# The gate and early merge weights of a two-layer hybrid encoder: their loads issued by ScalarE instead of SyncE

## The chip, the cores and the metric

The kernel runs on one core of a Trainium2 chip. A core has a matrix engine (TensorE, PE in the profile; its weight loads are PEld), VectorE (DVE), ScalarE (ACT), GpSimd (POOL) and SyncE (SP), which here only issues DMA transfers. Each engine executes its own instructions in order, and semaphores tie the engines together. ScalarE and GpSimd can issue DMA transfers too, as instructions among their others. The metric is the time of one execution on the device in microseconds (us); three executions of the kernel before took 3136.10, 3140.98 and 3143.68 us, median 3140.98.

## What is computed

Two layers of a bidirectional encoder trunk, sequence 2048, width 1024, float32. Cut to what matters:

```
for l in range(2):
    h = rms_norm(x, norm_w[l])
    qkv, z_a, a_lg, b_lg, cf_val, cf_glu, z_b, gate_lg = split(h @ w_in[l])
    # branch A: short convolution + SiLU on q, k, v; normalised q, k; the gated
    # delta rule in chunks of 64, forward and backward, both summed:
    #   v_new = value - k_cum @ S;  o = q_dec @ S + attn @ v_new
    #   S = S * decay + k_dec^T @ v_new
    o = rms_norm_per_head(o_fwd + o_bwd) * silu(z_a)
    y_a = o @ w_dn_out[l]
    # branch B: GLU, convolution of width 31, LayerNorm, SiLU, gated
    y_b = (u * silu(z_b)) @ w_cf_out[l]
    gate = sigmoid(gate_lg + gate_b)          # 2 x 1024 wide
    x = x + (gate[0] * y_a + gate[1] * y_b) @ w_out[l]
return rms_norm(x, final_norm_w)
```

The change concerns the weights of `gate_lg` (the last 2048 columns of `w_in`) and of `w_cf_out`.

## The kernel before

**Dense products.** A product of two float32 operands is made of three matrix products on reduced-precision parts: each operand is split into a high part and the rest, and PE forms high by high (L185), rest by high (L186) and high by rest (L187). A weight tile has 1024 (for `w_cf` 512) input rows and 128 output columns. `weight_parts` loads it in blocks of 512 rows, 128x512 numbers or 256 KB each, into the tile `wraw` (two buffers), so a gate weight takes two loads and a `w_cf` weight one. `split` then forms `whi` with a copy on ScalarE (L159) and `wlo` with a subtraction on VectorE (L160); both have two buffers. `weight` is `weight_parts` followed at once by the split. `load` and `store` issue on SyncE's queue (L147, L150), `astore` on ScalarE's (L153), `pstore` on GpSimd's.

**Stages of a layer.** First the input products with the short convolution, then the Conformer branch and the products of z. Then come the *early gates*, `gates(0)`: the gate products of the first half of the sequence, between which VectorE and GpSimd work on the Conformer convolution and its norm and on the triangular solves of the recurrence. Then `delta()`, the recurrence of branch A, in 16 steps, each for both directions. Last comes the merge with the rest of `w_cf`, with `w_dn` and `w_out`.

**The recurrence and its filler.** The steps of the recurrence are chains of small operations across PE, ScalarE and VectorE, so dense products are put between them as filler: `pull(n)` takes n pieces from a generator. `filler` first gives `gates(1)`, the gate products of the second half of the sequence, and after them `early_merge`, which multiplies half of branch B by `w_cf` and by its gate. A few pieces go into the *lead-in* ahead of step 0 (`LEAD`), 16 into each step (`STEP`, four times four), the rest behind. After delta(), `bind` makes the written order binding for PE, ScalarE, VectorE and GpSimd, while SyncE's loads are free to go ahead in the order that the scheduler found.

**A gate product** is 24 matmuls into a bank `pd` of PSUM (three banks), which ScalarE empties with the bias into `go` (L829); `astore` writes that to memory as `gt`. The recurrence's own results go into banks `pz`, five in turn.

**Lines of the recurrence that the text speaks of.** PE: L936 and L946 in the preparation of a later step; L989 and L992 apply the state, L1005, L1014 and L1023 give the step's output and the state's increment. ScalarE: L925 and L963 in the preparation, L939 there too, L998 and L1007 in the step itself. VectorE: transposes L917 and copies L971 and L972 in the preparation, L1017 for the state's update. When both directions of a pair of chunks are there (steps 8 to 15), `finish` squares their sum on ScalarE (L1044), forms the norms' factors with small operations on VectorE (from L1054), has the scaled sum transposed by PE into `pz`, and multiplies it by the z gate on VectorE (L1068), which empties that bank. In steps 8 to 11 (`LATE_SQUARES` = 12) these squares come ahead of the third `pull` of the step, later behind it:

```
            if step < LATE_SQUARES:
                next(new)
            pull(STEP[2])
            if step >= LATE_SQUARES:
                next(new)
```

Of the kernel before, what the change touches and what calls it, by code (L numbers as in the profile page):

```python
# [19 lines left out]
KD = 8  # L20
# [39 lines left out]
def sort(ps):  # L60
    return ps.rearrange("p (i a) -> p a i", a=2)


def cut(x):
    return x.rearrange("p (a i) -> p a i", a=2)
# [13 lines left out]
class Trunk:  # L79
# [78 lines left out]
    def split(self, hi, lo, src):  # L158
        self.nc.scalar.activation(hi, src, AF.Copy)  # L159
        self.nc.vector.tensor_tensor(out=lo, in0=src, in1=hi.bitcast(F32), op=ALU.subtract)  # L160

    def weight_parts(self, src, kk):
        hi = self.pw.tile([P, KD, P], F32R, tag="whi", bufs=2, name="whi")[:, 0:kk, :]
        lo = self.pw.tile([P, KD, P], F32R, tag="wlo", bufs=2, name="wlo")[:, 0:kk, :]
        raws = []
        for k in range(0, kk, 4):
            raws.append(self.pw.tile([P, 4, P], F32, tag="wraw", bufs=2, name="wraw"))
            self.load(raws[-1], src[:, k:k + 4, :])

        def split():  # L170
            for k, raw in zip(range(0, kk, 4), raws):
                self.split(hi[:, k:k + 4, :], lo[:, k:k + 4, :], raw)
        return (hi, lo), split

    def weight(self, src, kk):
        w, split = self.weight_parts(src, kk)
        split()
        return w

# [630 lines left out]
    def gates(self, half):  # L810
        nc = self.nc
        seq = [(j, b) for j in range(16) for b in range(2)]
        if half:
            seq = seq[:28] + [(14, 0), (15, 0), (14, 1), (15, 1)]
        ws = {}
        for i, (j, b) in enumerate(seq):
            for q, _ in seq[i:]:
                if q not in ws and len({z for z, _ in seq[i:] if z in ws}) < 2:
                    ws[q] = self.weight(self.a["w_in"][self.l, 28 + q], KD)
            blk = 2 * half + b  # L820
            ps = self.pd()
            for more in self.dense_steps(ps, ws[j], self.hx(blk), KD):
                if more:
                    yield 1
            if self.rate:
                self.follow()
                self.pump(self.rate)
            o = self.st("go")
            nc.scalar.activation(cut(o), sort(ps), AF.Identity if half else AF.Sigmoid,  # L829
                                 bias=self.vec[:, V_GB + j:V_GB + j + 1])  # L830
            self.astore(self.gt_d[j, :, blk * NB:(blk + 1) * NB], o)
            yield 1
# [321 lines left out]
    def filler(self):  # L1154
        wcf = self.a["w_cf"][self.l]
        seq = [(j, b) for j in range(KD) for b in range(2)]
        u = ahead = None
        gs = deque()

        def gate(i):  # L1160
            j, b = seq[i]
            t = self.st("g1")
            self.load(t, self.gt_d[8 + j][:, b * NB:(b + 1) * NB])
            gs.append(t)

        def units():
            yield from self.gates(1)
            self.u0 = u
            self.y1 = self.big([P, KD, HALF], F32, "y1")
            yield from self.early_merge(wcf, ahead, seq, gs, gate)  # L1170

        for n, v in enumerate(units()):
            yield v
            if n == 30 * KD - 1:
                self.drain()
                self.rate = 0.0
                u = self.big([P, 8, HALF], F32R, "uop")
                raw = lambda k, b: u[:, 4 + k, b * NB:(b + 1) * NB]
                for b in range(2):
                    for k in range(4):  # L1180
                        self.load(raw(k, b).bitcast(F32), self.u_d[k, :, b * NB:(b + 1) * NB])
                gate(0)
            if n == 31 * KD - 1:
                ahead = self.weight(wcf[0], 4)
                gate(1)
            if n in SPLITS:
                b, k = divmod(SPLITS.index(n), 4)
                self.split(u[:, k, b * NB:(b + 1) * NB], raw(k, b), raw(k, b).bitcast(F32))

    def early_merge(self, wcf, ahead, seq, gs, gate):  # L1190
        nc = self.nc
        for i, (j, b) in enumerate(seq):
            if b == 0:
                wc = ahead
                if j + 1 < KD:
                    ahead, split = self.weight_parts(wcf[j + 1], 4)
            elif j + 1 < KD:
                split()
            if i + 2 < len(seq):
                gate(i + 2)  # L1200
            g = gs.popleft()
            sl = slice(b * NB, (b + 1) * NB)
            ps = self.pd()
            for more in self.dense_steps(ps, wc, lambda k: (self.u0[:, k, sl], self.u0[:, 4 + k, sl]), 4):
                if more:
                    yield 1
            nc.vector.tensor_tensor(out=cut(self.y1[:, j, sl]), in0=sort(ps), in1=cut(g), op=ALU.mult)
            yield 1
# [291 lines left out]
```

## Time and profile before

| | before |
|---|---|
| median of three executions | 3140.98 us (3136.10 to 3143.68) |
| profiled execution | 3143.1 us |
| its span in the profile | 3141.3 us |
| mean granted clock of TensorE | 0.995 |
| busy PE / DVE / ACT / POOL | 3077.3 / 2400.3 / 1377.3 / 297.9 us |

The page gives busy time of each engine over the span. A row of the waits reads: engine, its tile and line, then the engine, tile and line that ended the wait; total us, times, longest. A row of the timeline reads: start in us from the start of the span, duration, engine, line, operation, out<-in with shapes, and how many instructions are drawn together; a wait ahead of it stands in brackets, with what ended it. ACTq and SPq are the issuing sides of the two DMA queues. A row of the transfers gives the number of issues, the size of one and the median time from issue to landing.

### The profile page before, as it was taken

The numbers are of one execution on the slowest core, as the hardware profiler recorded it, in microseconds if no ns is written. First come the engines' busy times: TensorE is split into PE (matmuls) and PEld (weight loads), VectorE is DVE, ScalarE is ACT, GpSimd is POOL, SyncE is SP. The second block draws the span as 40 slices with busy tenths as digits, with TensorE's granted clock in tenths as the row PEclk, the third lists the DMA queues.
The fourth block names the chain that finished last, engine by engine and source line by source line (L and its number), as shares of the span: only waits on it lengthen the run. The fifth ranks groups of instructions, "written<-read, shape, count | busy, mean of one in ns | idle before, by whom it ended". The sixth has DMA issues, their size and how long they took to land. (4 is left out here: it accounts for less than half of the span.)

```text
span 3141.3 us, 51438 instructions
## 1 busy us (share of the span) xinstructions
PE 3077.3 (98%) x19190; PEld 2707.1 (86%) x19190; DVE 2400.3 (76%) x4441; ACT 1377.3 (44%) x3074; POOL 297.9 (9%) x297
## 2 busy tenths in 40 slices
PE   6999999999999999999999999999999999999998
PEld 5888888888889998888888888888888899988887
DVE  7789898997556698746666989999955567877665
ACT  5625152522454466434345252525234545644342
POOL 3000000000032222000000000000001212200000
PEclk9999999999999999999999999999999999999999
DMA  4233222234587787655413141414347878965643
GB/s 147 90 95 95 88 91 91 89 111 137 194 297 253 250 266 237 198 188 141 152 35 106 67 124 58 121 61 119 124 158 258 269 234 266 290 201 189 216 159 124
DMA packets 429417, 501.71 MB, mean 160 GB/s; under 512 B 96432, under 2 KB 262960, under 8 KB 429168
## 3 DMA queue, kind: packets, MB, share of 16 engines
q1 hardware_dynamic: 351232, 380.19, 38.8%
q10 hardware_dynamic: 69872, 88.48, 8.0%
q0 software_dynamic: 8064, 29.76, 2.5%
q8 instruction: 151, 2.47, 0.3%
q14 instruction: 98, 0.80, 0.1%
HBM read 342.74 MB, written 155.58 MB: 159 GB/s over the span
## 5 line engine op out<-in xcount | busy, mean ns | idle before, releaser
L185 PE MATMUL pd<-h,whi 128*128 128x512 f32 x2816 | 1092.3, 388 | 0.0
L187 PE MATMUL pd<-h,wlo 128*128 128x512 f32 x2816 | 1070.5, 380 | 1.5 <-DVE wlo L160 1.5
L186 PE MATMUL pd<-h,whi 128*128 128x512 f32 x2816 | 1070.9, 380 | 0.0
L749 DVE SCALAR_TENSOR_TENSOR cacc<-gp,vec,cacc 128x1009 f32<-128x1009 f32 (+1 forms) x480 | 615.7, 1283 | 29.6 <-ACT cacc L747 26.6
L185 PEld LDWEIGHTS pd<-h,whi 128*128 128x128 f32 x2816 | 534.1, 190 | 79.5 <-issue 1.4
L187 PEld LDWEIGHTS pd<-h,wlo 128*128 128x128 f32 x2816 | 533.7, 190 | 78.6 <-DVE wlo L160 2.3
L186 PEld LDWEIGHTS pd<-h,whi 128*128 128x128 f32 x2816 | 534.0, 190 | 72.6 <-issue 1.9
L159 ACT ACTIVATE whi<-wraw 128x512 fp32r<-128x512 f32 x394 | 239.3, 623 | 478.6 <-PE pd L186 352.6
L160 DVE TENSOR_TENSOR wlo<-wraw,whi 128x512 fp32r<-128x512 f32 x394 | 267.8, 693 | 116.9 <-ACT whi L159 115.2
L574 DVE SCALAR_TENSOR_TENSOR acc<-cin,vec,acc 128x1022 f32<-128x1022 f32 (+1 forms) x192 | 246.5, 1299 | 13.9 <-ACT acc L572 12.6
L187 PE MATMUL pd<-yhi,wlo 128*128 128x512 f32 x488 | 185.6, 380 | 4.6 <-DVE wlo L160 4.5
L185 PE MATMUL pd<-yhi,whi 128*128 128x512 f32 x488 | 185.5, 380 | 0.7 <-ACT whi L159 0.7
L186 PE MATMUL pd<-ylo,whi 128*128 128x512 f32 x488 | 185.0, 379 | 0.0
L829 ACT ACTIVATE go<-pd,vec 128x512 f32<-128x512 f32 x128 | 87.3, 682 | 130.9 <-PE pd L187 116.6
L550 ACT ACTIVATE cin<-pd 128x512 f32<-128x512 f32 x96 | 56.8, 593 | 152.3 <-PE pd L187 152.1
L761 ACT ACTIVATE ao<-pd 128x512 f32<-128x512 f32 x64 | 38.3, 599 | 193.9 <-PE pd L187 193.8
L187 PEld LDWEIGHTS pd<-yhi,wlo 128*128 128x128 f32 x488 | 92.2, 189 | 19.5 <-DVE wlo L160 6.6
L185 PE MATMUL pd<-uop,whi 128*128 128x512 f32 x256 | 100.2, 391 | 5.1 <-ACT whi L159 5.1
L185 PEld LDWEIGHTS pd<-yhi,whi 128*128 128x128 f32 x488 | 92.2, 189 | 14.3 <-ACT whi L159 1.5
L186 PEld LDWEIGHTS pd<-ylo,whi 128*128 128x128 f32 x488 | 92.2, 189 | 12.9
L187 PE MATMUL pd<-uop,wlo 128*128 128x512 f32 x256 | 98.0, 383 | 0.1
L186 PE MATMUL pd<-uop,whi 128*128 128x512 f32 x256 | 97.8, 382 | 0.0
(312 smaller groups left out, 4814.9 us busy)
## 6 DMA issues: line engine op xcount, KB each, us to landing
wraw<-w_in SPq DMA_DIRECT2D x240, 256.0 KB, 3.5
gt<-go ACTq DMA_DIRECT2D x128, 256.0 KB, 4.2
dl<-gr SPq DMA_DIRECT2D x128, 256.0 KB, 5.3
dl<-kq SPq DMA_DIRECT2D x64, 512.0 KB, 6.3
dl<-kv SPq DMA_DIRECT2D x64, 512.0 KB, 5.7
wraw<-w_out SPq DMA_DIRECT2D x90, 256.0 KB, 3.0
kq<-acc SPq DMA_DIRECT2D x16, 1024.0 KB, 5.4
gr<-go ACTq DMA_DIRECT2D x64, 256.0 KB, 2.2
```

What stands on the lines that cost most here:

```text
L159: self.nc.scalar.activation(hi, src, AF.Copy)
L160: self.nc.vector.tensor_tensor(out=lo, in0=src, in1=hi.bitcast(F32), op=ALU.subtract)
L185: mm(ps, whi[:, k, :], xhi, start=k == 0, stop=False)
L186: mm(ps, whi[:, k, :], xlo, start=False, stop=False)
L187: mm(ps, wlo[:, k, :], xhi, start=False, stop=k == kk - 1)
L550: nc.scalar.activation(cut(t[:, o + b * NB:o + (b + 1) * NB]), sort(ps), AF.Copy)
L574: self.nc.vector.scalar_tensor_tensor(out=out, in0=t[:, k:k + n], scalar=wc(k), in1=out, op0=ALU.mult, op1=ALU.add)
L749: self.nc.vector.scalar_tensor_tensor(out=acc, in0=t[:, k:k + n], scalar=wc(k), in1=acc, op0=ALU.mult, op1=ALU.add)
L761: nc.scalar.activation(cut(o), sort(ps), func)
L829: nc.scalar.activation(cut(o), sort(ps), AF.Identity if half else AF.Sigmoid, bias=self.vec[:, V_GB + j:V_GB + j + 1])
```

## The change

`weight_parts` and `weight` take a queue, and three callers hand them `astore`: both calls of `gates` (64 loads per layer), the first `w_cf` weight in `filler`, and the seven that follow in `early_merge` (8 per layer). These 72 loads per layer, 144 in all, are issued by ScalarE instead of SyncE. All other weights, those of the input products, of `w_dn` and `w_out`, stay with SyncE, as do the tiles, their buffers, the splits and the products.

```diff
--- before.py
+++ after.py
@@ -159,21 +159,21 @@
         self.nc.scalar.activation(hi, src, AF.Copy)
         self.nc.vector.tensor_tensor(out=lo, in0=src, in1=hi.bitcast(F32), op=ALU.subtract)
 
-    def weight_parts(self, src, kk):
+    def weight_parts(self, src, kk, queue=None):
         hi = self.pw.tile([P, KD, P], F32R, tag="whi", bufs=2, name="whi")[:, 0:kk, :]
         lo = self.pw.tile([P, KD, P], F32R, tag="wlo", bufs=2, name="wlo")[:, 0:kk, :]
         raws = []
         for k in range(0, kk, 4):
             raws.append(self.pw.tile([P, 4, P], F32, tag="wraw", bufs=2, name="wraw"))
-            self.load(raws[-1], src[:, k:k + 4, :])
+            (queue or self.load)(raws[-1], src[:, k:k + 4, :])
 
         def split():
             for k, raw in zip(range(0, kk, 4), raws):
                 self.split(hi[:, k:k + 4, :], lo[:, k:k + 4, :], raw)
         return (hi, lo), split
 
-    def weight(self, src, kk):
-        w, split = self.weight_parts(src, kk)
+    def weight(self, src, kk, queue=None):
+        w, split = self.weight_parts(src, kk, queue)
         split()
         return w
 
@@ -816,7 +816,7 @@
         for i, (j, b) in enumerate(seq):
             for q, _ in seq[i:]:
                 if q not in ws and len({z for z, _ in seq[i:] if z in ws}) < 2:
-                    ws[q] = self.weight(self.a["w_in"][self.l, 28 + q], KD)
+                    ws[q] = self.weight(self.a["w_in"][self.l, 28 + q], KD, self.astore)
             blk = 2 * half + b
             ps = self.pd()
             for more in self.dense_steps(ps, ws[j], self.hx(blk), KD):
@@ -1181,7 +1181,7 @@
                         self.load(raw(k, b).bitcast(F32), self.u_d[k, :, b * NB:(b + 1) * NB])
                 gate(0)
             if n == 31 * KD - 1:
-                ahead = self.weight(wcf[0], 4)
+                ahead = self.weight(wcf[0], 4, self.astore)
                 gate(1)
             if n in SPLITS:
                 b, k = divmod(SPLITS.index(n), 4)
@@ -1193,7 +1193,7 @@
             if b == 0:
                 wc = ahead
                 if j + 1 < KD:
-                    ahead, split = self.weight_parts(wcf[j + 1], 4)
+                    ahead, split = self.weight_parts(wcf[j + 1], 4, self.astore)
             elif j + 1 < KD:
                 split()
             if i + 2 < len(seq):
```

What this does to the written order of ScalarE is seen at three places. First a step of the recurrence from 8 to 11, where finished chunks are squared (L1044), in the difference of the two orders:

```order
 L925 ACTIVATE dh_6988<-dh_6987 32x4x32 x4
 L1044 ACTIVATE junk,oss<-dm_6984 128x128 x8
+L153 DMA wraw<-w_in 128x512 x2
 L159 ACTIVATE whi<-wraw 128x512 x2
 L829 ACTIVATE go<-pd,vec 128x512
```

The issue of both halves of a weight now stands behind the squares and directly ahead of the two splits that read them. This place comes four times in a layer. In steps 0 to 7 it is the same without the squares, eight times in a layer:

```order
 L963 ACTIVATE dh_6989<-pz 128x256
 L925 ACTIVATE dh_6988<-dh_6987 32x4x32 x4
+L153 DMA wraw<-w_in 128x512 x2
 L159 ACTIVATE whi<-wraw 128x512 x2
 L829 ACTIVATE go<-pd,vec 128x512
```

Two more weights stand so in the lead-in, behind the store of a gate tile; the first of them with L939 of the preparation behind it:

```order
 L829 ACTIVATE go<-pd,vec 128x512
 L153 DMA gt_150<-go 128x512
+L153 DMA wraw<-w_in 128x512 x2
 L159 ACTIVATE whi<-wraw 128x512 x2
 L939 ACTIVATE dh_6989<-pz 128x128
```

The first `w_cf` weight goes the same way; for the other seven, L1044 or L1007 stands between issue and split. In the early gates the issue stands one or two ScalarE instructions ahead of a split of an earlier weight, and two splits and a `go` ahead of its own. On SyncE's side a plain step had, before:

```order
L147 DMA dl_6980<-kv_140 128x1024
L147 DMA dm_6982<-gc_143 128x512 x2
L147 DMA wraw<-w_in 128x512 x2
L147 DMA dl_6980<-kq_139 128x1024 x2
L147 DMA dh_6987<-inv_142 128x4x32 x2
```

and has now:

```order
L147 DMA dl_6980<-kv_140 128x1024
L147 DMA dm_6982<-gc_143 128x512 x2
L147 DMA dl_6980<-kq_139 128x1024 x2
L147 DMA dh_6987<-inv_142 128x4x32 x2
```

The weight's loads stood between the loads of the recurrence's operands for a later step; now these follow each other without them. The orders of PE and GpSimd are the same as before.

## The prediction

> **What bounds the kernel now.** I read the page's busy times first, then the list of what TensorE (PE) waited for, then busy time by stage, then the instructions of single steps in order of time.
>
> ```profile
> span 3141.3 us, 51438 instructions
> PE 3077.3 (98%) x19190; PEld 2707.1 (86%) x19190; DVE 2400.3 (76%) x4441; ACT 1377.3 (44%) x3074; POOL 297.9 (9%) x297
> ```
>
> PE is busy for 98% of the span and idle for 64 us in all. Anything that helps can only come out of those 64 us; anything that makes PE wait comes on top. The rows below are PE's waits that concern weights or the recurrence (total us, times, longest), and one row of SyncE's queue.
>
> ```profile
> PE pd L187 <- DVE wlo L160: 6.0, 5, 1.7
> PE pd L185 <- ACT whi L159: 5.8, 4, 2.7
> ...
> PE pz L946 <- ACT dh L939: 2.6, 2, 1.4
> ...
> PE pz L989 <- DVE dh L1068: 1.6, 2, 0.8
> ```
> ```profile
> SPq L147 <- DVE wlo L160: 731.0, 245, 53.3
> ```
>
> SyncE's queue stands 731 us waiting for weight buffers, but PE loses only 6.0 + 5.8 us to late weights in the whole run. That is the ceiling of what any weight load can give back. Now two stages of layer 0: plain steps 0 to 7 of the recurrence with gates as filler, and steps 8 to 11, in which each finished pair of chunks is squared as well.
>
> ```profile
> core 0: us, PE busy (x) PEld busy (x) DVE busy (x) ACT busy (x) POOL busy (x), PEclk, DMA share, GB/s
> 920.00:1098.00 178.00, 178.00 (x1930) 160.85 (x1926) 107.80 (x294) 81.17 (x225) 39.24 (x34) 1.00 0.79 252
> 1098.00:1192.00 94.00, 93.89 (x998) 84.95 (x993) 85.69 (x217) 62.47 (x210) 28.00 (x24) 1.00 0.85 264
> ```
>
> PE never rests in either part of the recurrence, but the others differ: VectorE (DVE) has 39% free in the plain steps and 9% (8.3 of 94 us) in the squaring steps. A delay put into VectorE's order is swallowed in the first and passed on in the second.
>
> **The change, part by part.** It takes 144 loads of 256 KB (64 gate halves and 8 merge weights per layer) from SyncE to ScalarE (ACT); bytes, splits and matmuls stay. In the early gates two splits stand between issue and use of most loads, so little changes. In the recurrence the orders shown above decide: 14 times per layer both halves of a weight are issued directly ahead of their own split. ScalarE then waits out the whole landing with everything behind it: go (which empties a pd bank), the gt store, L998, L939, L1007; and VectorE waits at wlo. Of the 14, two stand in the lead-in, eight in steps 0 to 7, four in steps 8 to 11. SyncE issued the same loads a step earlier, right after the previous wlo.
>
> How long a landing takes, from the loads of these weights in the recurrence (issues with the median; then min/median/max for the stretch 895 to 1205):
>
> ```profile
> wraw<-w_in SPq DMA_DIRECT2D x20, 256.0 KB, 5.3
> ```
> ```profile
> DMA to landing us min/median/max: 3.9/5.4/8.0
> ```
>
> No row shows such a load on ScalarE's queue. I take L = 5.3 us and keep 3.9 and 8.0 as its ends: the traffic beside it is the same, though it no longer stands behind SyncE's other loads.
>
> *Squaring steps.* First ScalarE, then VectorE, in step 9.
>
> ```profile
> 1126.07 1.13 ACT L159 ACTIVATE whi<-wraw 128x512 fp32r<-128x512 f32 x2
> ```
> ```profile
> 1121.11 0.49 DVE L917 STREAM_TRANSPOSE dh<-dh 128x128 f32<-128x128 f32 x2
> ...
> 1126.71 1.29 DVE L160 TENSOR_TENSOR wlo<-wraw,whi 128x512 fp32r<-128x512 f32 x2 [1.36 <-ACT whi L159]
> 1127.92 1.40 DVE L1068 SCALAR_TENSOR_TENSOR dh<-pz,vec,dh 128x512 f32<-128x512 f32 x2
> ...
> 1144.62 0.49 DVE L917 STREAM_TRANSPOSE dh<-dh 128x128 f32<-128x128 f32 x2
> ```
>
> This is a closed loop without slack: the transpose L917 releases ScalarE's L925, the squares L1044 follow, then whi, which wlo waits for (1.36 us), then VectorE runs without a gap through L1068, small operations on the norms and the state update L1017 to the next L917, 23.51 us later. Before, whi starts at 1126.07 and wlo ends at 1128.0. Changed, the loads are issued at 1126.07; the first lands at 1131.37, the pair of splits ends at 1132.5, wlo at 1133.2: 5.2 us later. L1068 stands right behind it, and PE already waits for L1068 (0.8 us, above), since it empties the bank that L989 needs. Step 8 has no L1068 yet but passes its lateness on through L917. So 4 x 5.2 = 20.8 us per layer; 4 x 3.8 = 15 and 4 x 7.9 = 32 at the ends.
>
> *Plain steps.* ScalarE, VectorE and PE in one of them:
>
> ```profile
> 988.77 1.15 ACT L159 ACTIVATE whi<-wraw 128x512 fp32r<-128x512 f32 x2
> 993.20 0.69 ACT L829 ACTIVATE go<-pd,vec 128x512 f32<-128x512 f32 x1 [3.28 <-PE pd L187]
> 993.91 0.33 ACTq L153 DMA_DIRECT2D gt<-go  x1
> ```
> ```profile
> 992.05 1.29 DVE L160 TENSOR_TENSOR wlo<-wraw,whi 128x512 fp32r<-128x512 f32 x2
> 993.67 0.43 DVE L972 COPY dl<-pz 64x256 f32<-64x256 f32 x1
> ```
> ```profile
> 996.66 0.45 PE L936 MATMUL pz<-dh,dl 32*32 32x32 f32 x32
> ```
>
> An issue costs ScalarE 0.33 us. Issued at 988.77, the loads land at 994.1 and 994.4; the splits end at 995.3, wlo at 996.0, L972 at 996.85. L972 empties the pz bank that L936 takes (five banks in turn, L936 five behind): PE waits 0.2 us. Up to 5.1 us of L nothing is lost, because ScalarE idled 3.28 us there and wlo came late anyway; at 8.0 us PE loses 2.9. I take 0.5 on average: 8 x 0.5 = 4 us per layer, ends 0 and 22. If L998 and L939 come late as well they still meet L1005's results, which come behind them.
>
> *Lead-in.*
>
> ```profile
> 892.28 0.33 ACTq L153 DMA_DIRECT2D gt<-go  x1
> 893.42 1.37 ACT L159 ACTIVATE whi<-wraw 128x512 fp32r<-128x512 f32 x2 [3.77 <-DMA wraw<-w_in]
> 894.69 0.26 ACT L939 ACTIVATE dh<-pz 128x128 f32<-128x128 f32 x1
> ```
> ```profile
> 895.01 0.23 PE L946 MATMUL pz<-dh,dh 32*32 32x32 f32 x4 [1.18 <-ACT dh L939]
> ...
> 910.81 1.95 PE L1005 MATMUL pz<-dl,dl 128*128 128x128 f32 x16
> ```
> ```profile
> 904.63 1.15 ACT L159 ACTIVATE whi<-wraw 128x512 fp32r<-128x512 f32 x2 [0.40 <-ACT go L829]
> ```
> ```profile
> 907.93 0.43 DVE L972 COPY dl<-pz 64x256 f32<-64x256 f32 x1
> ```
>
> L946 already waits on ScalarE here. The first load can go once the gt store ahead of it has gone: issue 892.6, landing 897.9, splits and L939 to 899.4, so PE stands 4.4 us longer; less if the store goes earlier. The second: 904.6, landings to 910.2, splits, wlo and L972 to 912.7 against L1005 at 910.81, 2 us or more. I take 4 + 3 = 7 per layer, ends 2 and 14.
>
> *Merge weights.* Only the first is issued directly ahead of its split; the others have squares or L1007 between.
>
> ```profile
> 1202.15 0.66 ACT L159 ACTIVATE whi<-wraw 128x512 fp32r<-128x512 f32 x1
> 1202.66 1.69 ACT L159 ACTIVATE uop<-uop 128x512 fp32r<-128x512 f32 x3
> 1204.97 0.60 ACT L1007 ACTIVATE dm<-pz 128x512 f32<-128x512 f32 x1 [0.62 <-PE pz L1005]
> ```
>
> With L, whi and uop end at 1202.15 + 5.3 + 0.6 + 1.7 = 1209.75, so L1007 is 4.8 us late, of which the filler behind L1005 covers some. I take 3, and 1 for the other seven: 4 per layer, ends 0 and 8.
>
> *Early gates.* Loads leave a queue that also holds the conformer norm's loads. Half of the 5.8 us that PE waited for whi may go: minus 1.5 per layer; ends minus 3, and plus 3 if ScalarE, now waiting for wlo at the issue, evicts late.
>
> *Clock.* In the page's finer slices one shows it falling:
>
> ```profile
> 2360.00:2400.00 40.00, 37.59 (x177) 32.27 (x176) 19.10 (x39) 16.47 (x25) 0.75 (x1) 0.96 0.61 207
> ```
>
> 2.4 us of idle time there cost 0.04 x 40 = 1.6 us of clock. In the squaring steps the loop, not PE, sets the pace, so I count it once per layer: 1.7 us. The Trainium skill (TensorE: Matmul & The Clock Gate, Part 1) has the clock halve after an idle window of about 3.4 us and stay so for about as long. By it, all eight long stalls could cost 1.7 us, 14 us in all instead of 3.4; the row, with less idle time than that, already shows a fall.
>
> Sum per layer: 20.8 + 4 + 7 + 4 - 1.5 + 1.7 = 36.0, twice 72 us. The profiled execution took 3143.1 us (span and 1.8 us around it), 2.1 above the median of the runs, 3140.98. So 3143.1 + 72 = 3215 in its terms, **3213 us** against the median.
>
> **The rivals.**
>
> *Worse: landings of 8 us.* The load can stand behind the gt store on ScalarE's queue, as in the lead-in, and its two halves share the engines with each other and with SyncE's loads. At L = 8.0: 32 + 22 + 14 + 8 = 76 per layer, about 3290; halfway, 3250. Against it: only the maxima are so long.
>
> *Mostly hidden: landings under 4 us.* On a queue that holds only stores: 15 + 0 + 2 + 1 - 3 = 15 per layer, 3171.
>
> *Faster.* SyncE, freed of 731 us of waiting, feeds gates and recurrence earlier, and PE gets back its waits for whi and L946: 5.8 + 2.6 = 8.4 us, 3133. It decides only where the landing is shorter than ScalarE's own idle time behind whi: 3.28 us in a plain step, and next to none in a squaring step. The shortest landing is 3.9.
>
> *Nothing.* Where a load starts does not matter: 3141. The Trainium skill (DMA: Bandwidth & Descriptors, Issuing engines are not separate DMA queues) says that DMAs of all queues share the same engines and that another issuer saves only issue time. By that rule alone nothing would change but 144 x 0.33 = 48 us of issue on an engine with 56% free. The trace agrees on the small issue cost; it speaks of transfers, not of what the issuer holds back while it waits.
>
> **How the numbers follow.** Forecast 0.62, worse 0.16, mostly hidden 0.12, faster 0.05, nothing 0.05. A measurement here tells 0.2% (6.3 us) from no change. Range 3165 to 3260: from the hidden case to a little beyond halfway to the worst. Faster 0.05, same 0.05, slower 0.90.
>
> **What would show it.** In the changed profile the row ACT whi waiting for DMA wraw<-w_in should grow by 100 us or more (28 landings of 5.3 us, less what it waits already), DVE wlo waiting for ACT whi should grow likewise, and PE should wait for DVE L1068 or L972 by some 5 us in three or four steps per layer; the stretch 1098 to 1192 should be about 21 us longer, the plain steps hardly. It is wrong if PE stays at 94 of 94 us in the squaring steps, if landings on ScalarE's queue are under 2 us, or if the loss sits in the early gates.

## The result, and the profile after

The changed kernel takes 3224.22 us (median of four executions, 3222.76 to 3227.22) against 3142.33 us for the kernel before on the same chip (3136.10 to 3144.66): 81.9 us slower, ratio 1.0265, 95% interval 1.0247 to 1.0283. The forecast was 3213, in the range 3165 to 3260, so 72 of the 82 us were expected.

The page of the changed kernel first, then its list of waits (engine, tile and line, what ended the wait; total us, times, longest).

```profile
span 3221.4 us, 51308 instructions
PE 3094.7 (96%) x19190; PEld 2719.7 (84%) x19190; DVE 2405.5 (75%) x4441; ACT 1376.1 (43%) x3074; POOL 297.8 (9%) x297
```
```profile
PE pz L989 <- DVE dh L1068: 32.0, 8, 5.7
PE pz L946 <- ACT dh L939: 16.8, 2, 9.3
...
PE pz L936 <- DVE dl L972: 11.9, 8, 3.2
...
PE pd L185 <- ACT whi L159: 7.3, 4, 3.0
...
PE pd L187 <- DVE wlo L160: 5.8, 5, 1.5
...
DVE wlo L160 <- ACT whi L159: 240.3, 108, 9.6
...
ACT whi L159 <- DMA wraw<-w_in: 220.3, 76, 9.1
...
SPq L147 <- DVE wlo L160: 588.9, 174, 51.5
```

The span grew by 80.1 us. PE's idle time went from 64.0 to 126.7 us and its busy time from 3077.3 to 3094.7 with the same number of instructions. Three rows account for 56.5 of the 62.7 us of new idle time: L989 behind L1068 (1.6 us before), L946 behind L939 (2.6) and L936 behind L972 (no row before). PE's own wait for a weight (L185 and L187) is as it was. The late weight is not what PE waits for; what it waits for stands behind the late weight on ScalarE and VectorE. The two signs that the prediction named for this, in the kernel before:

```profile
DVE wlo L160 <- ACT whi L159: 115.2, 71, 7.0
...
ACT whi L159 <- DMA wraw<-w_in: 74.8, 24, 10.0
```

They grew by 125 and 146 us, as foretold. SyncE waits 142 us less for weight buffers (731.0 before), and no gain from it shows.

To see in which stage the time went I compare the start of the first L1005 of each step in both traces (us that the changed kernel is behind; layer 0, layer 1):

| at | layer 0 | layer 1 | growth since the row above |
|---|---|---|---|
| last gate ahead of the lead-in | -1.5 | 36.4 | -1.5, and -4.2 from the end of layer 0's recurrence |
| step 0 | 8.0 | 48.0 | lead-in: 9.5 and 11.6 |
| step 8 | 12.2 | 50.9 | plain steps: 4.2 and 2.9 |
| step 12 | 37.1 | 75.2 | squaring steps: 24.9 and 24.3 |
| step 15 | 40.6 | 79.5 | merge weights: 3.5 and 4.3 |

(The first row is taken at the last L829 of the early gates. Of the 4.2 us in layer 1, 3.2 lie in its early gates.)

**A squaring step.** ScalarE, VectorE and PE of the changed kernel in step 9:

```profile
1142.38 0.35 ACTq L153 DMA_DIRECT2D wraw<-w_in  x1
...
1142.76 0.46 ACTq L153 DMA_DIRECT2D wraw<-w_in  x1
1147.52 0.63 ACT L159 ACTIVATE whi<-wraw 128x512 fp32r<-128x512 f32 x1 [4.75 <-DMA wraw<-w_in]
1148.40 0.63 ACT L159 ACTIVATE whi<-wraw 128x512 fp32r<-128x512 f32 x1 [0.25 <-DMA wraw<-w_in]
```
```profile
1148.18 0.69 DVE L160 TENSOR_TENSOR wlo<-wraw,whi 128x512 fp32r<-128x512 f32 x1 [6.26 <-ACT whi L159]
1149.06 0.69 DVE L160 TENSOR_TENSOR wlo<-wraw,whi 128x512 fp32r<-128x512 f32 x1 [0.19 <-ACT whi L159]
1149.67 1.40 DVE L1068 SCALAR_TENSOR_TENSOR dh<-pz,vec,dh 128x512 f32<-128x512 f32 x2
...
1166.73 0.49 DVE L917 STREAM_TRANSPOSE dh<-dh 128x128 f32<-128x128 f32 x2
```
```profile
1145.20 1.06 PE L992 MATMUL pz<-dh,dl 128*128 128x128 f32 x8
1150.47 1.84 PE L989 MATMUL pz<-dh,dl 128*128 128x128 f32 x8 [4.21 <-DVE dh L1068]
1152.11 1.91 PE L992 MATMUL pz<-dh,dl 128*128 128x128 f32 x8
```

The loads are issued as the squares end, the first half arrives 5.1 us later, VectorE stands 6.26 us instead of 1.36, L1068 follows at once, and PE stands 4.21 us for the bank that L1068 empties. Behind the stall eight matmuls take 1.84 and 1.91 us instead of 1.06: PE's clock has dropped. The granted clock (the third figure from the end) is 0.50 in this stretch:

```profile
1150.75:1154.16 3.41, 3.41 (x32) 3.19 (x35) 3.33 (x13) 0.51 (x3) 1.27 (x1) 0.50 0.65 199
```

**The lead-in.** ScalarE, then PE:

```profile
888.21 0.33 ACTq L153 DMA_DIRECT2D gt<-go  x1
891.20 2.04 ACTq L153 DMA_DIRECT2D wraw<-w_in  x2
897.28 0.63 ACT L159 ACTIVATE whi<-wraw 128x512 fp32r<-128x512 f32 x1 [9.10 <-DMA wraw<-w_in]
```
```profile
899.84 0.28 PE L946 MATMUL pz<-dh,dh 32*32 32x32 f32 x4 [7.49 <-ACT dh L939]
...
901.11 0.63 PE L186 MATMUL pd<-h,whi 128*128 128x512 f32 x1
...
905.20 0.38 PE L187 MATMUL pd<-h,wlo 128*128 128x512 f32 x1
```

PE stands 7.49 us at L946 (1.18 before), and then its matmuls take 0.63 us, until at 905.20 they are back at 0.38.

The two halves of the weight went out at 891.20 and 892.89, though the gt store ahead of them had been issued by 888.54. The trace's semaphore events tell why. Each transfer raises a completion semaphore when it lands; SyncE's and ScalarE's transfers raise the same eight, and each of these two issues waits for an earlier transfer that raises the same one. For the first half that is the gt store issued at 882.16, for the second SyncE's load `dl<-gr` issued at 881.16. The two transfers (number, size, us to landing):

```profile
gt<-go ACTq DMA_DIRECT2D x1, 256.0 KB, 9.0
```
```profile
dl<-gr SPq DMA_DIRECT2D x1, 256.0 KB, 11.7
```

They land at 891.18 and 892.87, 0.02 us ahead of the issues. ScalarE was held at the two issues for 2.7 and 1.4 us in this way, and for 1.9 and 4.6 us in layer 1.

How long the loads took from issue to landing in the steps (line L153, tile wraw, 925 to 1226 us; issues, then min/median/max), and busy time by stage with the granted clock (columns as in the prediction):

```profile
L153 ACTq DMA_DIRECT2D wraw<-w_in x24: 339/340/565, 928.4 to 1201.9; - x24
...
DMA to landing us min/median/max: 4.9/5.9/6.7
```
```profile
884.00:931.00 47.00, 38.86 (x376) 32.35 (x375) 20.12 (x42) 21.10 (x55) 10.37 (x9) 0.89 0.73 246
...
1113.00:1226.00 113.00, 96.10 (x952) 86.91 (x952) 81.37 (x203) 59.60 (x199) 27.97 (x24) 0.91 0.64 204
```

The landing is 5.9 us, not 5.3, and never 8. The granted clock is 0.89 around the lead-in and 0.91 in the squaring steps, where it had been 1.00.

### The profile page after: what moved, and what is told of

Its sections match the earlier page's. It is cut to its first block, busy times and chain, and to the rows that moved or that the text cites. A ratio compares the mean times of both kernels' runs of the same rounds, so it can differ in the third digit from the quotient of the medians.

```text
span 3221.4 us, 51308 instructions
## 1 busy us (share of the span) xinstructions
PE 3094.7 (96%) x19190; PEld 2719.7 (84%) x19190; DVE 2405.5 (75%) x4441; ACT 1376.1 (43%) x3074; POOL 297.8 (9%) x297
## 5 line engine op out<-in xcount | busy, mean ns | idle before, releaser
L185 PE MATMUL pd<-h,whi 128*128 128x512 f32 x2816 | 1094.9, 389 | 0.0
L187 PE MATMUL pd<-h,wlo 128*128 128x512 f32 x2816 | 1072.4, 381 | 1.5 <-DVE wlo L160 1.5
L185 PEld LDWEIGHTS pd<-h,whi 128*128 128x128 f32 x2816 | 535.7, 190 | 80.1 <-issue 1.4
L187 PEld LDWEIGHTS pd<-h,wlo 128*128 128x128 f32 x2816 | 534.8, 190 | 79.3 <-DVE wlo L160 2.3
L187 PE MATMUL pd<-yhi,wlo 128*128 128x512 f32 x488 | 185.7, 381 | 4.5 <-DVE wlo L160 4.3
L185 PE MATMUL pd<-yhi,whi 128*128 128x512 f32 x488 | 185.4, 380 | 0.5 <-ACT whi L159 0.5
L829 ACT ACTIVATE go<-pd,vec 128x512 f32<-128x512 f32 x128 | 87.0, 680 | 109.8 <-PE pd L187 39.1
L761 ACT ACTIVATE ao<-pd 128x512 f32<-128x512 f32 x64 | 38.3, 598 | 189.9 <-PE pd L187 185.7
L187 PEld LDWEIGHTS pd<-yhi,wlo 128*128 128x128 f32 x488 | 92.2, 189 | 19.6 <-DVE wlo L160 6.8
L185 PE MATMUL pd<-uop,whi 128*128 128x512 f32 x256 | 100.0, 391 | 6.8 <-ACT whi L159 6.8
L185 PEld LDWEIGHTS pd<-yhi,whi 128*128 128x128 f32 x488 | 92.2, 189 | 13.9 <-ACT whi L159 1.2
L989 PE MATMUL pz<-dh,dl 128*128 128x128 f32 x480 | 69.4, 291 | 32.0 <-DVE dh L1068 32.0
L187 PE MATMUL pd<-uop,wlo 128*128 128x512 f32 x256 | 98.3, 384 | 0.1
```

The lines of the kernel that those rows point to most:

```text
L185: mm(ps, whi[:, k, :], xhi, start=k == 0, stop=False)
L187: mm(ps, wlo[:, k, :], xhi, start=False, stop=k == kk - 1)
L761: nc.scalar.activation(cut(o), sort(ps), func)
L989: mm(pk[:, hd, :], kq[:, hd, 0, :], s[:, hd, :], start=True, stop=True)
```

## Experiments

The theory, from the forecast: an issue on ScalarE costs nothing by itself; time is lost where it stands directly ahead of its own split, because ScalarE then keeps back everything behind it for a landing, and most where the step is a closed loop through ScalarE and VectorE. The main rival: the queue costs, so that each load on it has its price, 82/144 = 0.57 us. Each difference below is against the kernel before on the same chip, medians, with the 95% interval of the ratio.

| kernel | loads on ScalarE | change, us | ratio (interval) |
|---|---|---|---|
| early gates only | 64 | -2.4 | 0.9990 (0.9982 to 0.9999) |
| recurrence's gates only | 64 | +74.0 | 1.0237 (1.0223 to 1.0250) |
| merge weights only | 16 | +8.2 | 1.0029 (1.0019 to 1.0039) |
| recurrence's gates, issued ahead | 56 | +7.7 | 1.0022 (1.0014 to 1.0031) |
| steps 8 to 11 only | 16 | +49.1 | 1.0151 (1.0131 to 1.0171) |
| none; ScalarE held, 8 copies | 0 | +24.7 | 1.0073 (1.0053 to 1.0093) |
| none; ScalarE held, 16 copies | 0 | +53.2 | 1.0159 (1.0135 to 1.0184) |
| recurrence's gates on GpSimd | 0 (64 there) | +10.1 | 1.0024 (1.0014 to 1.0034) |
| lead-in only | 8 | +19.4 | 1.0065 (1.0049 to 1.0080) |
| steps 0 to 7 only | 32 | +15.1 | 1.0052 (1.0038 to 1.0066) |
| early gates, and steps issued ahead | 112 | -2.2 | 0.9992 (0.9983 to 1.0001) |

### The three parts of the change, each alone

The edit against the changed kernel is the queue handed over (w_cf back to SyncE in the first two):

```diff
-                    ws[q] = self.weight(self.a["w_in"][self.l, 28 + q], KD, self.astore)
+                    ws[q] = self.weight(self.a["w_in"][self.l, 28 + q], KD, None if half else self.astore)   # early gates only
+                    ws[q] = self.weight(self.a["w_in"][self.l, 28 + q], KD, self.astore if half else None)   # recurrence only
+                    ws[q] = self.weight(self.a["w_in"][self.l, 28 + q], KD, None)                            # merge weights only
```

> Only the 64 gate loads (32 per layer) of the early gates are issued by ScalarE; the recurrence's gate weights and w_cf stay with SyncE. Theory (ScalarE is held where a load stands directly ahead of its own split, elsewhere nothing is lost): in the changed profile the early gates came 1.5 and 3.2 us earlier, so this is 3 to 6 us faster or not to be told from no change, 3136 to 3140 against 3142. Rival (every load on ScalarE's queue costs by itself, 82 us / 144 loads = 0.57 us each): 64 x 0.57 = 36 us slower, 3178.

> Only the 64 gate loads of the recurrence (gates(1)) are issued by ScalarE. Theory: nearly the whole loss, that of lead-in, plain and squaring steps as read off the changed profile, about 33 us in layer 0 and 36 in layer 1: 3205 to 3215. Rival of a price per load: 64 x 0.57 = 36 us slower, 3178.

> Only the 16 loads of w_cf (8 per layer) in the early merge are issued by ScalarE. Theory: the part behind step 11, which the changed profile shows 5.9 and 5.7 us longer: 3148 to 3156, or less where part of that was inherited from the squaring steps. Rival of a price per load: 9 us, 3151, not told apart by this run alone.

Measured: -2.4, +74.0 and +8.2 us. The recurrence's gates alone came out 2.8 us above the range that I had given. The three parts add up to 79.8 of the 81.9 us, so no effect of one on another shows. The two halves of the gate weights are the same 64 loads of the same size on the same queue, and one can hardly be told from no change while the other costs 74 us. A price per load is out.

### The recurrence's loads on ScalarE, issued ahead of time

From the third weight on, the loads of the next weight are issued behind the gt store of the tile before; the splits stay where they were. Early gates and w_cf are as before the change. Two helpers carry it:

```diff
-                    ws[q] = self.weight(self.a["w_in"][self.l, 28 + q], KD)
+                    ws[q] = late_split(self, early.pop(q)) if q in early else self.weight(self.a["w_in"][self.l, 28 + q], KD)
...
-            yield 1
+            yield raw_ahead(self, half, ws, early)
...
+def raw_ahead(self, half, ws, early):
+    q = max(ws) + 1
+    if half and q < 16 and q not in early:
+        early[q] = []
+        for k in range(0, KD, 4):
+            early[q].append(self.pw.tile([P, 4, P], F32, tag="wraw", bufs=2, name="wraw"))
+            self.astore(early[q][-1], self.a["w_in"][self.l, 28 + q][:, k:k + 4, :])
+    return 1
```

> The recurrence's gate weights from the third on are issued by ScalarE's queue, but right behind the gt store of the tile before, about half a step or more ahead of their split, which stays where it was; early gates and w_cf as before, on SyncE. Theory (the place costs, not the queue): within 6 us of before, 3136 to 3148, and ScalarE's wait for the weights in the recurrence is gone. Rival (the queue costs: shared completions, SyncE's loads and ScalarE's colliding): 3178 by the price per load, up to 3210 if as much as with the loads ahead of their splits.

Measured: +7.7 us instead of +74. In a squaring step of this kernel ScalarE reads

```profile
1127.00 1.13 ACT L159 ACTIVATE whi<-wraw 128x512 fp32r<-128x512 f32 x2
1128.16 0.69 ACT L829 ACTIVATE go<-pd,vec 128x512 f32<-128x512 f32 x1
1128.88 0.33 ACTq L153 DMA_DIRECT2D gt<-go  x1
1129.31 1.68 ACTq L153 DMA_DIRECT2D wraw<-w_in  x2
```

Both splits run without a wait, and PE's wait at L989 is back to 2.1 us in all. By the starts of L1005 the steps lose 0.6 us in layer 0 and 0.2 in layer 1. The median landing of these loads in the steps is 5.4 us, against 5.9 in the changed kernel: nearly as long, only nobody stands behind it. The 7.7 us are more than the 6 that the theory allowed. The trace puts them ahead of step 0, with a wait of ScalarE at its first L913 and one of PE:

```profile
885.09 1.28 ACT L913 ACT_TABLE_LOAD   x1 [4.65 <-DMA dl<-kv]
```
```profile
PE pz L936 <- DVE dl L927: 7.4, 4, 3.4
```

L913 stands behind an issue, L927 behind L913, and L936 behind L927. The issue is that of the second half of a weight; its rows, and the transfer whose semaphore it waited for, a SyncE load issued at 876.48 that landed at 884.59:

```profile
880.89 4.12 ACTq L153 DMA_DIRECT2D wraw<-w_in  x2
```
```profile
dl<-kv SPq DMA_DIRECT2D x1, 512.0 KB, 8.1
```

The second half went at 884.66, after 3.2 us of holding ScalarE; layer 1 shows the same with 3.5 us. So what remains is in the main a cost of the queue after all, in a form that the rival named: the two queues share their completion semaphores. This is read from the trace; a kernel with separate semaphores was not run. The last kernel below takes the lead-in's two weights out of it.

### How ScalarE being held becomes time

Here the opposite: all loads with SyncE as before, but in steps 8 to 11 ScalarE copies a 128x128 tile into a scratch tile, 8 or 16 times, between the squares and the split; the copies compute nothing.

```diff
-                    ws[q] = self.weight(self.a["w_in"][self.l, 28 + q], KD)
+                    ws[q] = held(self, 8 if half and q >= 12 else 0, self.weight_parts(self.a["w_in"][self.l, 28 + q], KD))
...
+def held(self, n, parts):
+    for _ in range(n):
+        self.nc.scalar.activation(self.junk, self.ident, AF.Copy)
+    parts[1]()
+    return parts[0]
```

> The kernel before with all loads on SyncE, but in steps 8 to 11 ScalarE does eight idle 128x128 copies (0.306 us each by the row of L913, 2.45 us) between the squares and the split; they write to a scratch tile and compute nothing. Theory (a closed loop through ScalarE without slack): 8 steps x 2.45 = 20 us, about 3163; PE's stalls at L989 are then about 2.5 us long and its clock stays near 1.00 in the squaring steps, PE busy within 5 us of before. Rival (the loss comes from the transfers on ScalarE's queue, not from ScalarE being held): 3144. Rival (the loop has some slack): clearly under 20 us.

> The same with sixteen idle copies, 4.9 us, about what the landing adds in the changed kernel. Theory: 8 x 4.9 = 39 us, about 3183, twice the step of eight copies, and like the loads of steps 8 to 11 alone; PE's stalls at L989 of about 5 us, its granted clock in the squaring steps down to some 0.91 as in the changed kernel, PE busy some 13 us more than before. Rival (transfers): 3144. Rival (slack): more than twice the loss of eight copies.

Measured: +24.7 and +53.2 us. First the kernel with 8 copies: ScalarE in one step, busy time in the stretch of steps 8 to 11 (the granted clock is the figure 0.97), and PE at two of its stalls. Then the one with 16: ScalarE, VectorE and PE.

```profile
1128.31 2.70 ACT L1504 ACTIVATE junk<-con 128x128 bf16<-128x128 f32 x8
```
```profile
1098.00:1204.00 106.00, 97.23 (x998) 87.62 (x995) 86.26 (x220) 72.74 (x245) 27.96 (x24) 0.97 0.75 235
```
```profile
1160.15 1.16 PE L989 MATMUL pz<-dh,dl 128*128 128x128 f32 x8 [1.67 <-DVE dh L1068]
...
1186.36 2.08 PE L989 MATMUL pz<-dh,dl 128*128 128x128 f32 x8 [2.84 <-DVE dh L1068]
```
```profile
1130.64 5.43 ACT L1504 ACTIVATE junk<-con 128x128 bf16<-128x128 f32 x16
```
```profile
1136.62 1.29 DVE L160 TENSOR_TENSOR wlo<-wraw,whi 128x512 fp32r<-128x512 f32 x2 [6.83 <-ACT whi L159]
```
```profile
1167.84 2.08 PE L989 MATMUL pz<-dh,dl 128*128 128x128 f32 x8 [4.40 <-DVE dh L1068]
```

A copy takes 0.34 us here, so whi comes 2.73 and 5.46 us later. The time from one L917 to the next, in layer 0, was 22.80, 23.51, 23.49 and 23.48 us before; it is 24.90, 26.58, 26.21 and 26.60 with 8 copies and 27.52, 29.22, 29.81 and 30.26 with 16. That is 11.0 us for 4 x 2.73 = 10.9 held, and 23.5 for 4 x 5.46 = 21.8. So the loop has no slack, and no transfer is needed for the loss. Of the rest, 1.2 us of layer 0 come in step 12 in both. My expectation was too low in part because I took a copy at 0.306 us. PE is busy 6.4 us longer with 8 copies and 16.1 with 16. I had expected no clock loss with 8. Of the three long stalls at L989 in layer 0, that of 1.67 us left the clock whole; those of 2.84 and 3.30 us did not.

### Only the squaring steps, only the lead-in, only the plain steps

```diff
-                    ws[q] = self.weight(self.a["w_in"][self.l, 28 + q], KD, self.astore)
+                    ws[q] = self.weight(self.a["w_in"][self.l, 28 + q], KD, self.astore if half and q >= 12 else None)       # steps 8 to 11
+                    ws[q] = self.weight(self.a["w_in"][self.l, 28 + q], KD, self.astore if half and q in (2, 3) else None)   # lead-in
+                    ws[q] = self.weight(self.a["w_in"][self.l, 28 + q], KD, self.astore if half and 4 <= q < 12 else None)   # steps 0 to 7
```

> Only the gate weights of steps 8 to 11 (16 loads, 8 per layer) are issued by ScalarE, all others by SyncE. Theory: the share of these steps as read off the changed profile, 19.5 and 19.9 us: 3143 + 39 = 3182, half of the whole change by a ninth of its loads. Rival of a price per load: 16 x 0.57 = 9 us, 3152.

> Only the two gate weights of the lead-in (the third and fourth of gates(1), 8 loads in all) are issued by ScalarE. Theory: PE stands at L946 for 7 to 9 us in each layer and is slow for some 2 us behind it, as in the changed profile; 11 us per layer or 22 us, 3165. Rival of a price per load: 8 x 0.57 = 5 us, 3148. Rival (those waits in the changed kernel come from the other loads on ScalarE's queue in the early gates): under 5 us as well.

> Only the eight gate weights of steps 0 to 7 per layer (32 loads in all) are issued by ScalarE. Theory: mostly covered, since ScalarE and VectorE have idle time there; by the changed profile 3 us per layer, by the remainder of the other runs (74 - 49 for steps 8 to 11 - 22 for the lead-in) about 3 in all: 3146 to 3152. Rival of a price per load: 32 x 0.57 = 18 us, 3161.

Measured: +49.1, +19.4 and +15.1 us. PE's waits, one row of each kernel in this order:

```profile
PE pz L989 <- DVE dh L1068: 31.2, 8, 5.4
```
```profile
PE pz L946 <- ACT dh L939: 15.8, 2, 8.3
```
```profile
PE pz L936 <- DVE dl L972: 10.5, 11, 1.6
```

Each part brings the wait that the forecast named for it. Sixteen loads in the squaring steps cost about 3 us each, thirty-two in the plain steps 0.5, and sixty-four in the early gates nothing. The three add up to 83.6 us, 9.6 more than the recurrence's gates together (+74.0); the four intervals, put together, leave about 10 us open, so this is not told from adding up. The starts of L1005 agree: alone the lead-in grows by 9.7 us in each layer, the plain steps by 6.7 and 4.6, the squaring steps by 25.0 and 23.4, 79.1 in all, and in the kernel with all three the same stretches grow by 80.3 (8.6 and 10.6, 2.7 and 3.5, 28.7 and 26.2). Together the plain steps lose less and the squaring steps more; why is not shown. My expectations for the squaring steps (39) and the plain steps (5 to 10) were read from marks on VectorE that the change itself moves within a step, and were too low. For the plain steps the price per load (18) came nearer than the theory; it is the other kernels that exclude it.

### The same loads issued by GpSimd

```diff
+                    ws[q] = self.weight(self.a["w_in"][self.l, 28 + q], KD, self.pstore if half else None)
```

> The 64 gate loads of the recurrence are issued by GpSimd at the same places of the program instead of by ScalarE; GpSimd is busy for only 9% and its order lets it reach the issue ahead of time, as SyncE does. Theory (what counts is whether the engine that issues is also held in front of the split): most of the 74 us is gone, 3142 to 3160, with a remainder where L907 or L875 behind the issue on GpSimd wait for wlo. Rival (any queue but SyncE's costs): as with ScalarE, near 3218.

Measured: +10.1 us, where ScalarE cost 74. GpSimd reaches the issue in step 9 at 1136.70, some 15 us ahead of the split, and nothing waits for the landing. By the starts of L1005 all of the loss in the sixteen steps, 3.8 us per layer, lies in the squaring steps. (Layer 1's lead-in is 2.7 us longer as well, but so it is, by 2.8 and 2.3, with 16 copies and with the squaring steps only, where it was not changed.) VectorE and GpSimd in step 9:

```profile
1136.88 3.49 DVE L205 TENSOR_TENSOR rst<-orr,rsv 128x8 f32<-128x8 f32 x1
1140.41 0.17 DVE L206 TENSOR_TENSOR rst<-rst,orr 128x8 f32<-128x8 f32 x1
```
```profile
1136.70 1.11 POOL L156 DMA_DIRECT2D wraw<-w_in  x2
1137.83 2.51 POOL L907 TENSOR_TENSOR dm<-dm,con 128x512 f32<-128x512 f32 x2
```

A VectorE operation of 0.17 us takes 3.49 and ends together with GpSimd's L907. The Trainium skill (SBUF — State Buffer, SBUF: two separate sides) says that a VectorE operation with two SBUF inputs and a GpSimd operation that reads SBUF exclude one another for a whole instruction; this row agrees in kind, though here the wait lasts through the rest of the issues and two GpSimd operations. In the kernel before, the same small operations (L1054 to L1058) were slow as well beside L875 and L907, and took from 1132.20 to 1139.48; now they take 1.3 us longer, and so does the step. The remainder that I had expected was another one, L907 or L875 waiting for wlo.

### The version with what costs nothing

Early gates as in the change, the recurrence's loads issued ahead as above but only from the fifth weight on, the lead-in's two weights and w_cf with SyncE:

```diff
-    if half and q < 16 and q not in early:
+    if half and 4 <= q < 16 and q not in early:
...
-                    ws[q] = late_split(self, early.pop(q)) if q in early else self.weight(self.a["w_in"][self.l, 28 + q], KD)
+                    ws[q] = late_split(self, early.pop(q)) if q in early else self.weight(self.a["w_in"][self.l, 28 + q], KD, None if half else self.astore)
```

> ScalarE issues the loads of the early gates as in the change, and those of the recurrence from the fifth weight on, but behind the gt store of the tile before, half a step ahead of their split; the lead-in's two weights and w_cf stay with SyncE. That is 112 of the 144 loads on ScalarE's queue. Theory: as the early gates alone, 3138 to 3143, since the 7.7 us that the recurrence's loads still cost when issued ahead all arose in the lead-in. Rival of a price per load: 112 x 0.57 = 64 us; rival (the 7.7 us belong to the steps): 3147 or more.

Measured: -2.2 us, like the early gates alone. So 112 of the 144 loads can go to ScalarE's queue without a loss that shows, and the 7.7 us of the loads issued ahead belonged to the lead-in. Neither this nor the early gates alone is better than the kernel before by more than 0.1% in the median.

## Why the prediction was right, point by point

Per layer the sum was 36.0 us; the stages grew by 40.6 and 38.9, with the clock's loss inside them.

- **The bound.** PE had 11.8 us of waits for weights to give back, and they did not move (13.1 after). Everything else came on top, as forecast.
- **Squaring steps, 20.8 us per layer.** Right in place and mechanism; 24.9 and 24.3 measured. The end of wlo, counted from the L917 ahead of it, came 4.9, 5.2, 5.6 and 6.1 us later in layer 0, 21.8 in all: that is the landing, 5.9 us where I had 5.3. Behind wlo the loop itself grew by 2.0 us, and the rest, about 1, came in step 12. Holding ScalarE without any transfer shows the same: one to one for 2.73 us, 1.08 to one for 5.46.
- **Plain steps, 4 us.** 4.2 and 2.9, by L972 and L936 as foreseen: six of the eight waits of that row, 6.4 of the 11.9 us, lie ahead of step 8, the other two in squaring steps. The size was a choice between 0 and 22, so that it fits so well is partly luck; alone these steps cost 6.7 and 4.6.
- **Lead-in, 4 + 3 = 7 us.** 9.5 and 11.6: the term was mis-sized. I let the load go at once behind the gt store; its two halves were held back by 2.7 and 1.4 us, until a store and a SyncE load with the same completion semaphores had landed. The forecast had no such wait. PE's wait at L946 grew by 6.3 us in layer 0, and its slow matmuls add some 2 (eleven starts from 900.52 to 904.95, 0.4 us apart instead of 0.21). The second weight, forecast at 3, cost less than 1: a wait of 0.6 us at the first L1005 in layer 0, 0.9 in layer 1.
- **Merge weights, 4 us.** 3.5 and 4.3, and 8.2 for both layers alone.
- **Early gates, -1.5 us.** Hardly shown. Counted from the last L761 ahead of them to their last L829, the early gates came out 0.7 us shorter in layer 0 and 3.3 in layer 1, but in the kernels that left them with SyncE the same stretches lie between -0.5 and 0.6, and between -2.4 and 1.1. That leaves 0.2 and 0.9 us beyond the scatter; -2.4 for both layers alone is at the edge of what can be told.
- **Clock, 1.7 us.** Mis-sized: PE was busy 17.4 us longer, 8.7 per layer. I had taken one slice with 2.4 us of idle time as the measure and counted it once per layer. There were six stalls of 4.2 to 5.7 us at L989 and two of 7.5 and 9.3 at L946, and the granted clock stood at half for 58 us in the two recurrences with their lead-ins, where it had not fallen at all before. This loss is part of the stages' rows above and does not come on top of them, as it did in my sum. The Trainium skill (TensorE: Matmul & The Clock Gate, Part 1) would have the clock halve after about 3.4 us of idle time for about as long; the estimate of 14 us that the prediction worked out by it is nearer to the 17.4 than the 3.4 of my row. Not all of it reached the end, since VectorE sets the pace of these steps: in step 9 it took 17.06 us from L1068 to L917 against 16.70, in spite of the slow matmuls.
- **The rivals.** Landings of 8 us did not come in the steps (6.7 at most), nor landings under 4. Of a gain no more showed than what stands at the early gates. That the place of an issue does not matter is wrong. That the queue itself costs nothing comes near the truth, with 112 loads on it at -2.2 us, but not all the way: in the lead-in a shared completion semaphore holds ScalarE, which accounts for most of the +7.7 us of the 56 loads issued ahead.

## What to carry to other kernels

A load that a compute engine issues holds that engine little longer than its issue if the consumer comes later in its order, and for a whole landing if the consumer is next; so look in the written order for what stands between issue and use, and behind the use. The issue itself can stand too, until an earlier transfer that raises the same completion semaphore has landed, be it one of another queue; in the lead-in that held ScalarE for some 3 to 6 us per layer. Price it by step: where the step is a loop through that engine without idle time, a delay passes one to one, and where the engine idles anyway it is mostly covered. PE's stalls of some 3 us and more also cost clock behind them; that belongs in the sum, once per stall.

## What the runs showed of the hardware

- The granted clock of TensorE is either 1.0 or 0.5 in these traces, and within the recurrences it stood at 0.5 in spells of 3.41, 6.83 or 10.24 us: once, twice or three times 3.41. Each PE stall above 3.1 us, the first 100 and the last 60 us of the traces left out, was accompanied or followed by such a spell. Between 1.6 and 3.1 us it varied: 1.71 us at 1277.11 with 8 copies was followed by one, 3.02 us at 2882.43 of the changed kernel was not.
- A DMA issue on ScalarE waited for earlier transfers with the same completion semaphore, its own queue's or SyncE's, for up to 4.6 us (2469.68 in the changed kernel).
- Small VectorE operations of 0.17 us took up to 3.49 us while GpSimd worked, and the squaring steps, whose pace VectorE sets, became 1.3 us longer by a change that only gave GpSimd another 1.1 us of work.
